# Key buffers in the sliding-window attention, output weights in halves, and the last norm on VectorE

## The chip, the cores and the metric

The kernel runs on one core of one Trainium2 chip. The metric is the device time of one execution in microseconds (us). Before the change it is 1278.24 us, the median of three runs (1277.53 to 1279.88).

## The reference

One decoder layer for a sequence of 1024 rows with 1024 columns, in float32. What is computed, cut to what matters here:

```
h    = rmsnorm(x) * (1 + sc1) + sh1              # sc1 .. g2 come from c @ w_ada
proj = h @ w_in                                  # columns for four groups of heads
o_sb = stick_breaking_attention(...)             # group 0
o_sw = sliding_window_attention(...)             # group 1: window 128, 4 query heads, 2 key heads
o_fx = forgetting_attention(...)                 # group 2
o_sm = s5_ssm(...)                               # group 3
mixed = rmsnorm per group of concat(o_sb, o_sw, o_fx, o_sm), each 256 wide
x = x + g1 * (mixed @ w_out)
h = rmsnorm(x) * (1 + sc2) + sh2
x = x + g2 * (square(relu(h @ w_mlp_in)) @ w_mlp_out)
return rmsnorm(x) * final_gain
```

## The kernel before

Products run on TensorE (PE) in three passes: each float32 operand is split into a high part (a rounded copy, made on ScalarE) and a low part (the difference, made on VectorE), and `mm3` adds high x high, high x low and low x high into one PSUM bank. PE, PEld, DVE, ACT, POOL and SP stand for TensorE's matmuls, its weight loads, VectorE, ScalarE, GpSimd and SyncE. The code is written in program order; a scheduler of the framework then sets the order in which each engine's instructions stand, and each engine takes them strictly in that order. SP issues nearly all loads and stores from one queue, again in a fixed order: an entry that has to wait for a buffer holds up every entry behind it.

Three places matter here.

The sliding-window attention (`sw_units`, from line 746) goes through eight units (j, p): j counts four pairs of row blocks, p the two key heads. For each j two key tiles `kk` (line 754, tag `kw`, two buffers in all) are loaded, one for each p (L756), and the query tiles `s` (L610). The scores are L733 on PE, their row maxima and exponentials L735 and L740. The units are mixed in with the end of the forgetting attention, with the projections of the groups 0 and 2 through `w_out` (L253 to L255 into `ps`, added to `x1` by L1029), and with the end of the state-space group (L831 to L913).

The output weights (`out_weights`, from line 969): for each of the groups 0, 2, 3 and 1, two blocks of 128 rows of `w_out` are loaded whole (128 x 1024, L975) into the tile `raw`, of which there is one buffer. VectorE multiplies the block by the gate g1 (L976), ScalarE copies the high part (L977), VectorE subtracts (L978). Only then is `raw` free for the next load. The squares of the second norm (`norm2`, L1139 and L98) use the same buffer.

The end: the last of 16 pieces of the hidden layer is multiplied for all eight row blocks t (the loop that calls `take` and `finish`). For each t and each half n, PE fills one bank with six matmuls, `take` adds it to `acc[t]` on VectorE (L1362), and `finish(t)` makes the last norm: squares with a running sum on ScalarE (L1385, by halves), a chain of six operations on 128 x 1 tiles on VectorE and two on ScalarE for the row factor (L1386, L86 to L92), and then the scaling by row factor and `final_gain`. For odd t VectorE does this in one instruction a half (L1390, `scalar_tensor_tensor`); for even t ScalarE scales (L1393) and GpSimd multiplies (L1394). Each half is stored by SP (L1395).

Of the kernel before, what the change touches and what calls it, by code (L numbers as in the profile page):

```python
# [9 lines left out]
F32 = mybir.dt.float32  # L10
F32R = mybir.dt.float32r
BF16 = mybir.dt.bfloat16
I32 = mybir.dt.int32
AF = mybir.ActivationFunctionType
ALU = mybir.AluOpType
# [4 lines left out]
P = 128  # L20
S = 1024
D = 1024
# [11 lines left out]
def tile_trunk(ctx: ExitStack, tc: tile.TileContext, a: dict, out: bass.AP):  # L34
    nc = tc.nc
    V, A, G, T, SY = nc.vector, nc.scalar, nc.gpsimd, nc.tensor, nc.sync
# [44 lines left out]
    def rsqrt_mean(pool, ss, n, width, tag, bufs=2):  # L81

        v = pool.tile([P, width], F32, name=f"{tag}v", tag=f"{tag}v", bufs=bufs)
        r = pool.tile([P, width], F32, name=f"{tag}r", tag=f"{tag}r", bufs=bufs)
        t = pool.tile([P, width], F32, name=f"{tag}t", tag=f"{tag}t", bufs=bufs)
        V.tensor_scalar(v, ss, 1.0 / n, EPS, op0=ALU.mult, op1=ALU.add)  # L86
        A.activation(r, v, AF.Ln)
        A.activation(r, r, AF.Exp, scale=-0.5)
        V.tensor_tensor(t, r, r, op=ALU.mult)
        V.tensor_tensor(t, t, v, op=ALU.mult)  # L90
        V.tensor_scalar(t, t, -0.5, 1.5, op0=ALU.mult, op1=ALU.add)
        V.tensor_tensor(r, r, t, op=ALU.mult)  # L92
        return r

    def norm_rows(pool, xt, sq, tag):

        ss = pool.tile([P, 1], F32, tag=f"{tag}ss", name="ss", bufs=2)
        A.activation(sq, xt, AF.Square, accum_out=ss)  # L98
        return rsqrt_mean(pool, ss, D, 1, tag)
# [1 line left out]
    WB, WA, XB, XQ = 5, 7, 4, 1  # L101
    RW, RC, LA, WS, FIRST, EB = 2, 6, 4, 2, 2, 4
    LB, RH = 2, 8
    FD_DVE, EL = (1, 3, 5, 7), 2
    MS = [5, 5, 5, 1]
    RC2 = max(MS) + LB + 1
    MARK = (1, 3)
# [497 lines left out]
    def load_q(qd, h, c0, c1):  # L605

        s = []
        for r in range(2):
            s.append(att.tile([P, c1 - c0], F32R, tag=f"s{r}", bufs=QB, name=f"s{r}"))
            load = SY.dma_start(out=s[r].bitcast(F32), in_=qd[h * HD:h * HD + HD, r:r + 2, c0:c1])  # L610
        return s, load.ins
# [112 lines left out]
    def sw_rows(q, kk, i, r, B, p):  # L724

        K = 256 if i else P
        z = ps1.tile([P, 2, 256], F32, tag="z", bufs=NZ, name="z")
        w = att.tile([P, 2, 256], F32, tag="t", bufs=3, name="w")
        m = att.tile([P, 4, 2], F32, tag="m", bufs=4, name="m")
        hs = slice(2 * p, 2 * p + 2)  # L730
        for x in range(2):
            for k in range(2):
                T.matmul(z[:, x, :], q[x][0][k][:, (i % 2) * P:(i % 2) * P + P], kk[:, 0:256],  # L733
                         start=k == 0, stop=k == 1)
            V.tensor_tensor_reduce(out=w[:, x, 0:K], in0=z[:, x, 0:K], in1=B[:, x, 256 - K:256], scale=1.0,  # L735
                                   scalar=-3e38, op0=ALU.add, op1=ALU.max, accum_out=m[:, 0, x:x + 1])
        V.scalar_tensor_tensor(out=m[:, 1], in0=m[:, 0], scalar=-1.0, in1=nsink[:, hs], op0=ALU.mult, op1=ALU.min)
        V.tensor_tensor(m[:, 2], m[:, 1], nsink[:, hs], op=ALU.subtract)
        for x in range(2):
            A.activation(w[:, x, 0:K], w[:, x, 0:K], AF.Exp, bias=m[:, 1, x:x + 1], accum_out=m[:, 3, x:x + 1])  # L740
        A.activation(m[:, 2], m[:, 2], AF.Exp)
        V.tensor_tensor(m[:, 3], m[:, 3], m[:, 2], op=ALU.add)
        V.reciprocal(r[:, i % 2], m[:, 3])
        return w

    def sw_units():

        B = [op.tile([P, 2, 256], F32, tag="B", bufs=2, name="B") for _ in range(2)]
        for b, t in enumerate(B):
            SY.dma_start(out=t, in_=BD[b])  # L750
        for j in range(4):
            k0 = max(2 * j - 1, 0) * P
            k1 = min(k0 + 384, S)
            kk = [op.tile([P, 384], F32R, tag="kw", bufs=2, name="kk") for _ in range(2)]
            for h in range(2):
                SY.dma_start(out=kk[h][:, 0:k1 - k0].bitcast(F32), in_=KD[2][h * HD:h * HD + HD, :, k0:k1])  # L756
            for p in range(2):
                q = [load_q(QD[2 + p], x, j * 256, j * 256 + 256) for x in range(2)]
                pv, r = None, att.tile([P, 2, 2], F32, tag="r", bufs=3, name="r")
                hs = slice(p * HD, p * HD + HD)  # L760
                for i in (2 * j, 2 * j + 1):
                    b0 = max(i - 1, 0)
                    w = sw_rows(q, kk[p][:, b0 * P - k0:], i, r, B[p], p)
                    ws = [[(w[:, x, (b - b0) * P:(b - b0 + 1) * P], b) for b in range(b0, i + 1)] for x in range(2)]
                    pv = mix(ws, v_sw, [hs, hs], i, pv, True)
                put(o_sw[:, 2 * j:2 * j + 2, p * P:p * P + P], pv, r)
                yield
# [198 lines left out]
    g1bc = op.tile([P, D], F32, name="g1bc")  # L966
    SY.dma_start(out=g1bc, in_=MD[2].to_broadcast([P, D]))

    def out_weights(g):

        h = op.tile([P, 2, D], F32R, tag="wo", bufs=4, name="woh")
        l = op.tile([P, 2, D], F32R, tag="wo", bufs=4, name="wol")
        for b in range(2):
            raw = op.tile([P, D], F32, tag="raw", bufs=1, name="raw")
            SY.dma_start(out=raw, in_=a["w_out"][0, g * 256 + b * P:g * 256 + b * P + P, :])  # L975
            V.tensor_tensor(raw, raw, g1bc, op=ALU.mult)  # L976
            A.copy(h[:, b], raw)  # L977
            V.tensor_tensor(l[:, b], raw, h[:, b], op=ALU.subtract)  # L978
        return h, l

    turns = [0]
# [70 lines left out]
    xts = [(xpa if n < 2 else xp).tile([P, 2, D], F32, name=f"x1_{n}") for n in range(4)]  # L1052
# [27 lines left out]
    def bank(kind):  # L1080
        n = used[kind] % 4
        used[kind] += 1
        pool, tag, bufs = ((ps2, "h", 3) if n < 3 else (psm, "ss", 1)) if kind == "x" else (
            (ps2, "t", 2) if n < 2 else (psm, "mm", 2))
        return pool.tile([P, 512], F32, tag=tag, bufs=bufs, name=kind)
# [49 lines left out]
    def norm2(j, y):  # L1135

        SY.dma_start(out=XD[j].rearrange("(t p) d -> p t d", p=P), in_=xts[j])
        for t in range(2):
            sq = op.tile([P, D], F32, tag="raw", bufs=1, name="sq")  # L1139
            r = norm_rows(op, xts[j][:, t], sq, "n2")  # L1140
            V.tensor_scalar(y[:, t], xts[j][:, t], r[:, 0:1], None, op0=ALU.mult)
        return [y[:, 0], y[:, 1]]

# [30 lines left out]
    for _ in range(FIRST):  # L1174
        x, z = bank("x"), bank("y")
        product(x, next_parts(), b11, True)
        product(z, next_parts(), b21, True)
        r = copy_of(x)
# [18 lines left out]
    for i in range(FIRST):  # L1197
        y = bank("y")
        product(y, next_parts(), t1, True)
        banks[i] += (y, copy_of(y))  # L1200
    for k, (u, b) in enumerate(zip(us, bs)):
        f = tt.tile([P, 512], F32, tag="f", bufs=2, name="f")
# [74 lines left out]
    for i in range(NP):  # L1277
        if i < FIRST:
            x, r, y, pe = banks[i]
            hidden(i, 0, r)  # L1280
        else:
            x, z, y = bank("x"), bank("y"), bank("y")
# [28 lines left out]
    sx = tc.alloc_tile_pool(name="sx", bufs=1, side="right", reuse_waits="tile")  # L1311
    acc = [sx.tile([P, D], F32, name=f"acc{t}") for t in range(NT)]
    g2bc = sx.tile([P, D], F32, name="g2bc")
    fg = sx.tile([P, D], F32, name="fg")
# [60 lines left out]
        V.tensor_tensor(acc[t][:, cs], acc[t][:, cs], g2bc[:, cs], op=ALU.mult)  # L1375
        V.tensor_tensor(acc[t][:, cs], acc[t][:, cs], rest_of[t][:, cs], op=ALU.add)

    def finish(t):

        y = acc[t]  # L1380
        ss = sx.tile([P, 2], F32, tag="n3ss", bufs=2, name="ss")
        halves = [slice(n * 512, n * 512 + 512) for n in range(2)]
        for n, cs in enumerate(halves):
            sq = sx.tile([P, 512], F32, tag="sq", bufs=2, name="sq")
            A.activation(sq, y[:, cs], AF.Square, accum_out=ss[:, n:n + 1])  # L1385
        V.tensor_tensor(ss[:, 0:1], ss[:, 0:1], ss[:, 1:2], op=ALU.add)  # L1386
        r = rsqrt_mean(sx, ss[:, 0:1], D, 1, "n3")
        for n, cs in enumerate(halves):
            if t in FD_DVE:
                V.scalar_tensor_tensor(out=y[:, cs], in0=y[:, cs], scalar=r[:, 0:1], in1=fg[:, cs],  # L1390
                                       op0=ALU.mult, op1=ALU.mult)
            else:
                A.activation(y[:, cs], y[:, cs], AF.Copy, scale=r[:, 0:1])  # L1393
                G.tensor_tensor(y[:, cs], y[:, cs], fg[:, cs], op=ALU.mult)  # L1394
            SY.dma_start(out=out[t * P:(t + 1) * P, cs], in_=y[:, cs])  # L1395

    last = load_raw(chunks[0], (0, 2, 1, 3)).ins
    for _ in range(RH):
# [28 lines left out]
    for t in range(NT):  # L1427
        for n in range(2):
            ps = bank("x" if n else "y")
            for x in range(2):  # L1430
                h = ha[2 * x + t // 4]
                ts = slice(t % 4 * P, t % 4 * P + P)
                mm3(ps, (h[0][:, ts], h[1][:, ts]), wa[2 * x + n], x == 0, x == 1)
            take(c, t, n, ps)
        finish(t)
    sr.release()
    sc.release()
    sr1.release()
# [52 lines left out]
```

## Time and profile before

| | |
|---|---|
| median of three runs | 1278.24 us |
| profiled execution | 1281.41 us, of which span 1279.3 us |
| PE busy | 1214.4 us (95%) |
| VectorE busy | 955.3 us (75%) |
| ScalarE busy | 562.4 us (44%) |
| GpSimd busy | 125.3 us (10%) |
| mean granted clock of TensorE | 0.976 of full speed |

The span runs from the first to the last instruction of the profiled execution; about 2.1 us lie around it. The clock is given as a share of the full 2.4 GHz; the other level is 1.2 GHz, 0.5. Matmuls are pipelined, so an instruction's own duration (0.39 us for one of 512 columns) is longer than the distance to the next (0.23 us). On VectorE, too, the distance between two independent instructions is shorter than the duration of one.

### The profile page before, as it was taken

How to read it: one execution, taken by the hardware profiler on the slowest of the kernel's cores; microseconds unless marked ns; L12 is line 12 of the kernel's file. 1: busy time of each engine (PE TensorE's matmuls, PEld its weight loads, DVE VectorE, ACT ScalarE, POOL GpSimd, SP SyncE). 2: the span in 40 equal slices, each digit the busy share in tenths (PEclk: the TensorE clock that was granted, in tenths of full speed). 3: DMA queues.
4: the chain of work that ended last, by engine and by line, in shares of the span. 5: the costliest groups of instructions: out<-in, count | busy, mean ns of one | idle time of the engine just before them, and what ended most of it. 6: DMA issues, size and time to landing. Idle time of an engine off the chain costs nothing.

```text
span 1279.3 us, 18741 instructions
## 1 busy us (share of the span) xinstructions
PE 1214.4 (95%) x6461; PEld 945.6 (74%) x6461; DVE 955.3 (75%) x2100; ACT 562.4 (44%) x1205; POOL 125.3 (10%) x171
## 2 busy tenths in 40 slices
PE   5899899999999998999899999999989999999994
PEld 3578677665677776888668888888867888888883
DVE  4685977775465687888998677767666777788998
ACT  4433555762224557545563232333344543433425
POOL 1218100000020100000000000000031210100003
PEclk9999899999999898999989999999999999999997
DMA  8664376576654655202124553443578653643413
GB/s 297 201 198 146 139 195 212 175 221 185 215 175 153 238 152 175 88 26 83 67 66 166 172 167 131 155 154 130 170 250 315 213 168 108 182 127 91 138 48 132
DMA packets 139334, 205.37 MB, mean 161 GB/s; under 512 B 37057, under 2 KB 77912, under 8 KB 139240
## 3 DMA queue, kind: packets, MB, share of 16 engines
q1 hardware_dynamic: 129768, 170.62, 41.6%
q0 software_dynamic: 9472, 33.56, 8.4%
q8 instruction: 51, 0.84, 0.3%
q14 instruction: 43, 0.35, 0.1%
HBM read 144.59 MB, written 59.55 MB: 160 GB/s over the span
## 4 chain that ended last, share of the span: by engine, by line
PE 80%; DVE 8%; DMA 7%; ACT 2%; issue 2%; SPq 1%; DVEq 0%; ACTq 0%
PE x L255 9%; PE x L253 9%; PE x L254 8%; PE y L254 6%; PE y L255 6%; PE y L253 6%; PE ps L253 6%; PE ps L254 6%; PE ps L255 6%; PE pv L705 3%; PE tp L700 3%; PE z L639 3%; PE ps L307 2%; DMA wa<-in_w_ada_dram 2%; DMA kk<-kd 1%
## 5 line engine op out<-in xcount | busy, mean ns | idle before, releaser
L1091 ACT CAST hi<-s 128x512 fp32r<-128x512 f32 x124 | 75.9, 618 | 110.8 <-PE x L254 36.7
L1091 ACT CAST hi<-hid 128x512 fp32r<-128x512 f32 x101 | 62.2, 618 | 129.7 <-issue 58.1
L254 PE MATMUL x<-lo,hi 128*128 128x512 f32 x256 | 98.3, 389 | 0.3 <-DVE lo L1092 0.3
L253 PE MATMUL x<-hi 128*128 128x512 f32 x256 | 95.9, 390 | 2.4 <-ACT hi L1091 2.4
L255 PE MATMUL x<-hi,lo 128*128 128x512 f32 x256 | 97.8, 389 | 0.0
L1092 DVE TENSOR_TENSOR lo<-raw,hi 128x512 fp32r<-128x512 f32 x97 | 65.9, 686 | 40.8 <-PE x L255 21.6
L253 PE MATMUL ps<-hT_hi,wh 128*128 128x512 f32 x224 | 90.8, 417 | 4.9 <-DVE e L273 2.6
L255 PE MATMUL ps<-hT_hi,wl 128*128 128x512 f32 x224 | 91.5, 411 | 1.5 <-DVE wl L185 1.5
L1091 ACT CAST hi<-raw 128x512 fp32r<-128x512 f32 x97 | 59.1, 619 | 74.2 <-PE y L254 45.9
L254 PE MATMUL ps<-hT_lo,wh 128*128 128x512 f32 x224 | 91.2, 408 | 0.0
L1092 DVE TENSOR_TENSOR lo<-s,hi 128x512 fp32r<-128x512 f32 x124 | 84.2, 684 | 3.1 <-ACT hi L1091 2.1
L1092 DVE TENSOR_TENSOR lo<-hid,hi 128x512 fp32r<-128x512 f32 x101 | 69.1, 685 | 21.1 <-ACT hi L1091 19.0
L255 PE MATMUL y<-hi,lo 128*128 128x512 f32 x196 | 75.3, 389 | 0.0
L254 PE MATMUL y<-lo,hi 128*128 128x512 f32 x196 | 75.2, 389 | 0.0
L253 PE MATMUL y<-hi 128*128 128x512 f32 x196 | 73.6, 390 | 0.3 <-ACT hi L1091 0.3
L700 PE MATMUL tp<-ident,w 128*128 128x128 f32 x348 | 60.3, 288 | 5.7 <-ACT w L666 5.5
L703 DVE COPY wt<-tp 128x512 f32<-128x512 f32 (+1 forms) x68 | 42.8, 638 | 27.2 <-PE tp L700 25.7
L1273 POOL DMA_DIRECT2D raw<-in_w_mlp_out_dram x64 | 34.4, 540 | 258.6 <-DVE lo L1092 75.1
L1099 POOL DMA_DIRECT2D raw<-in_w_mlp_in_dram x16 | 14.4, 898 | 453.9 <-DVE lo L1092 384.9
L253 PEld LDWEIGHTS x<-hi 128*128 128x128 f32 x256 | 48.0, 188 | 13.1 <-ACT hi L1091 3.2
L639 PE MATMUL z<-kk,s 128*128 128x256 f32 (+2 forms) x192 | 55.2, 382 | 2.5 <-DMA kk<-kd 2.5
L700 PEld LDWEIGHTS tp<-ident,w 128*128 128x128 f32 x348 | 40.0, 144 | 23.8 <-issue 11.2
(416 smaller groups left out, 3261.2 us busy)
## 6 DMA issues: line engine op xcount, KB each, us to landing
hid<-hh SPq DMA_DIRECT2D x101, 256.0 KB
wa<-in_w_ada_dram SPq DMA_DIRECT2D x32, 512.0 KB
raw<-in_w_mlp_in_dram POOLq DMA_DIRECT2D x16, 1024.0 KB, 7.0
raw<-in_w_mlp_out_dram POOLq DMA_DIRECT2D x64, 256.0 KB, 4.5
hh<-x SPq DMA_DIRECT2D x60, 256.0 KB
hh<-h SPq DMA_DIRECT2D x49, 256.0 KB
s<-qd SPq DMA_DIRECT2D x96, 128.0 KB
wa<-in_w_ada_dram SPq DMA_DIRECT2D x32, 256.0 KB
```

The costliest lines, as they stand in the source:

```text
L253: T.matmul(ps, wh, xh, start=first, skip_group_check=more, stop=False)
L254: T.matmul(ps, wh, xl, start=False, skip_group_check=more, stop=False)
L255: T.matmul(ps, wl, xh, start=False, skip_group_check=more, stop=last)
L307: T.matmul(ps[32 * r:32 * r + 1, :], cact[:, k:k + 1], w[:, n * 512:(n + 1) * 512], start=k == 0, stop=k == KT - 1)
L639: T.matmul(z[:, 0:n], q[r][:, qs], kk[:, 0:n], start=r == 0, stop=stop and r == 1)
L700: T.transpose(tp[:, b, :], w, ident)
L703: (A.copy if copies[0] % 2 and both else V.tensor_copy)(wt[:, 0:len(part)], tp[:, 0:len(part)])
L705: T.matmul(pv[x * HD:x * HD + HD, i % 2, :], v[:, kb, hs[x]], wt[:, b, :], start=n == 0, stop=n == len(ws[0]) - 1)
L1091: A.copy(shape(hi), src)
L1092: V.tensor_tensor(shape(lo), src, shape(hi), op=ALU.subtract)
L1099: G.dma_start(out=raws[i].rearrange("p (k c) -> p k c", k=KT), in_=w1[:, i * 256:i * 256 + 256].rearrange("(k p) c -> p k c", p=P))
L1273: load = G.dma_start(out=raw2[i, kind], in_=w2[(2 * i + x) * P:(2 * i + x + 1) * P, n * 512:n * 512 + 512])
```

## The change

1. `sw_units`: the key tiles `kk` have three buffers instead of two. A tile is then free for its next load when the scores of the unit three loads earlier are done, not two loads earlier.
2. `out_weights`: each block is loaded, multiplied, copied and subtracted in two halves of 512 columns, and `raw` has two buffers of half the size. `norm2` squares in two halves too, and adds the two sums.
3. `finish`: all eight row blocks are scaled on VectorE by `scalar_tensor_tensor`; ScalarE's scaling and GpSimd's multiplication are gone. The row factors of two blocks are made by one chain on 128 x 2 tiles for the pairs (0, 1), (2, 3), (4, 5); the blocks 6 and 7 have a chain each.

```
-            kk = [op.tile([P, 384], F32R, tag="kw", bufs=2, name="kk") for _ in range(2)]
+            kk = [op.tile([P, 384], F32R, tag="kw", bufs=3, name="kk") for _ in range(2)]
...
-            raw = op.tile([P, D], F32, tag="raw", bufs=1, name="raw")
-            SY.dma_start(out=raw, in_=a["w_out"][0, g * 256 + b * P:g * 256 + b * P + P, :])
-            V.tensor_tensor(raw, raw, g1bc, op=ALU.mult)
-            A.copy(h[:, b], raw)
-            V.tensor_tensor(l[:, b], raw, h[:, b], op=ALU.subtract)
+            for n in range(2):
+                ns = slice(n * 512, n * 512 + 512)
+                raw = op.tile([P, 512], F32, tag="raw", bufs=2, name="raw")
+                SY.dma_start(out=raw, in_=a["w_out"][0, g * 256 + b * P:g * 256 + b * P + P, ns])
+                V.tensor_tensor(raw, raw, g1bc[:, ns], op=ALU.mult)
+                A.copy(h[:, b, ns], raw)
+                V.tensor_tensor(l[:, b, ns], raw, h[:, b, ns], op=ALU.subtract)
...
-            sq = op.tile([P, D], F32, tag="raw", bufs=1, name="sq")
-            r = norm_rows(op, xts[j][:, t], sq, "n2")
+            ss = op.tile([P, 2], F32, tag="n2ss", bufs=2, name="ss")
+            for n in range(2):
+                sq = op.tile([P, 512], F32, tag="raw", bufs=2, name="sq")
+                A.activation(sq, xts[j][:, t, n * 512:n * 512 + 512], AF.Square, accum_out=ss[:, n:n + 1])
+            V.tensor_tensor(ss[:, 0:1], ss[:, 0:1], ss[:, 1:2], op=ALU.add)
+            r = rsqrt_mean(op, ss[:, 0:1], D, 1, "n2")
...
-    def finish(t):
+    def finish(ts):
...
+        n = len(ts)
+        ss = sx.tile([P, 2, 2], F32, tag="n3ss", bufs=2, name="ss")
+        for x, t in enumerate(ts):
+            for h in range(2):
+                sq = sx.tile([P, 512], F32, tag="sq", bufs=2, name="sq")
+                A.activation(sq, acc[t][:, h * 512:h * 512 + 512], AF.Square, accum_out=ss[:, h, x:x + 1])
+        V.tensor_tensor(ss[:, 0, 0:n], ss[:, 0, 0:n], ss[:, 1, 0:n], op=ALU.add)
+        r = rsqrt_mean(sx, ss[:, 0, 0:n], D, n, f"n3{n}")
+        for x, t in enumerate(ts):
+            for h in range(2):
+                cs = slice(h * 512, h * 512 + 512)
+                y = acc[t][:, cs]
+                V.scalar_tensor_tensor(out=y, in0=y, scalar=r[:, x:x + 1], in1=fg[:, cs], op0=ALU.mult, op1=ALU.mult)
+                SY.dma_start(out=out[t * P:(t + 1) * P, cs], in_=y)
...
-        finish(t)
+        if t % 2 or t == 6:
+            finish({1: (0, 1), 3: (2, 3), 5: (4, 5)}.get(t, (t,)))
```

The scheduler's order is the same up to the first of the new loads and again in the two MLP products; it differs from there to the second norm and in the end. Three places follow.

First, SP's queue while the sliding-window units run. Before the change, `kk_5700`, the key tile of the unit j=2, p=0, stands behind the queries of the unit after its own (`s0_5776` to `s0_5780`) and between the stores of the state-space group's third and second output piece (`o_4065`, `o_4080`):

```order
L913 DMA od2_74<-o_4065 128x256
L913 DMA od3_75<-o_4065 128x256
L610 DMA s0_5776<-qd3_64 128x1x256
L610 DMA s1_5778<-qd3_64 128x1x256
L610 DMA s0_5780<-qd3_64 128x1x256
L756 DMA kk_5700<-kd2_69 128x384
L913 DMA od0_72<-o_4080 128x256
L913 DMA od1_73<-o_4080 128x256
L610 DMA s1_5782<-qd3_64 128x1x256
```

After the change the same entry stands directly behind the queries of the unit j=1, p=1 (`s0_5632`, `s1_5634`) and ahead of the first store of the state-space group (`o_4050`):

```order
L977 DMA raw_6536<-in_w_out_dram 128x512
L977 DMA raw_6541<-in_w_out_dram 128x512
L610 DMA s0_5632<-qd3_64 128x1x256
L610 DMA s1_5634<-qd3_64 128x1x256
L756 DMA kk_5700<-kd2_69 128x384
L913 DMA od0_72<-o_4050 128x256
L913 DMA od1_73<-o_4050 128x256
L610 DMA s0_5704<-qd2_63 128x1x256
L913 DMA od2_74<-o_4065 128x256
L913 DMA od3_75<-o_4065 128x256
L610 DMA s1_5706<-qd2_63 128x1x256
L610 DMA s0_5708<-qd2_63 128x1x256
```

The load has moved ahead of four stores and seven loads of queries that stood in front of it, and it now waits for the scores of unit j=0, p=1 instead of those of unit j=1, p=0.

Second, VectorE's order where the second block of group 3's weights is made. Before the change, the multiplication of the whole block stands 23 rows behind the subtraction that frees its buffer; these are the last ten of them:

```order
L92 TENSOR_TENSOR gnr<-gnr,gnt 128x2
L742 TENSOR_TENSOR m<-m 128x2
L721 TENSOR_TENSOR o_sw<-pv,rb 128x2x128
L743 RECIPROCAL r<-m 128x2
L735 ISA w,m<-z,B 128x256
L735 ISA m 128x1
L715 COPY rw<-r 128x256
L735 ISA w,m<-z,B 128x256
L735 ISA m 128x1
L976 TENSOR_TENSOR raw<-raw,g1bc 128x1024
```

After the change, the multiplication of the first half (L978 there) stands eleven rows behind the two subtractions (L980) that free the two buffers:

```order
L980 TENSOR_TENSOR wol<-raw,woh 128x512 x2
L735 ISA w,m<-z,B 128x256
L735 ISA m 128x1
L735 ISA w,m<-z,B 128x256
L735 ISA m 128x1
L742 TENSOR_TENSOR m<-m 128x2
L721 TENSOR_TENSOR o_sw<-pv,rb 128x2x128
L86 TENSOR_SCALAR gnv<-ps 128x2
L737 SCALAR_TENSOR_TENSOR m<-m,nsink 128x2
L743 RECIPROCAL r<-m 128x2
L738 TENSOR_TENSOR m<-m,nsink 128x2
L978 TENSOR_TENSOR raw<-raw,g1bc 128x512
```

Less of VectorE's work stands between the freeing of the buffer and the use of what is loaded into it.

Third, the end of VectorE's order (`acc_9864` and `acc_9866` are the row blocks 5 and 7). Before the change the chains of the row factors of blocks 6 and 7 run side by side, and only block 7 is scaled here:

```order
L1390 SCALAR_TENSOR_TENSOR acc_9864<-acc_9864,n3r,fg 128x512 x2
L1386 TENSOR_TENSOR ss<-ss 128x1
L89 TENSOR_TENSOR n3t<-n3r 128x1
L86 TENSOR_SCALAR n3v<-ss 128x1
L90 TENSOR_TENSOR n3t<-n3t,n3v 128x1
L91 TENSOR_SCALAR n3t<-n3t 128x1
L92 TENSOR_TENSOR n3r<-n3r,n3t 128x1
L89 TENSOR_TENSOR n3t<-n3r 128x1
L90 TENSOR_TENSOR n3t<-n3t,n3v 128x1
L91 TENSOR_SCALAR n3t<-n3t 128x1
L92 TENSOR_TENSOR n3r<-n3r,n3t 128x1
L1390 SCALAR_TENSOR_TENSOR acc_9866<-acc_9866,n3r,fg 128x512 x2
```

After the change (`acc_9929` and `acc_9930` are the blocks 6 and 7) the scaling of block 6 stands inside the chain of block 7:

```order
L1392 TENSOR_TENSOR ss<-ss 128x1
L89 TENSOR_TENSOR n31t<-n31r 128x1
L86 TENSOR_SCALAR n31v<-ss 128x1
L90 TENSOR_TENSOR n31t<-n31t,n31v 128x1
L91 TENSOR_SCALAR n31t<-n31t 128x1
L92 TENSOR_TENSOR n31r<-n31r,n31t 128x1
L89 TENSOR_TENSOR n31t<-n31r 128x1
L1398 SCALAR_TENSOR_TENSOR acc_9929<-acc_9929,n31r,fg 128x512 x2
L90 TENSOR_TENSOR n31t<-n31t,n31v 128x1
L91 TENSOR_SCALAR n31t<-n31t 128x1
L92 TENSOR_TENSOR n31r<-n31r,n31t 128x1
L1398 SCALAR_TENSOR_TENSOR acc_9930<-acc_9930,n31r,fg 128x512 x2
```

Directly in front of these rows now stand the four scalings of the blocks 4 and 5, and in front of those the two `take`s of block 7.

## Rows read from the trace of the kernel before

**Rows 1.** The page: busy time by engine, and the chain's shares.

```profile
PE 1214.4 (95%) x6461; PEld 945.6 (74%) x6461; DVE 955.3 (75%) x2100; ACT 562.4 (44%) x1205; POOL 125.3 (10%) x171
PE 80%; DVE 8%; DMA 7%; ACT 2%; issue 2%; SPq 1%; DVEq 0%; ACTq 0%
```

**Rows 2.** Windows: length, busy PE, PEld, DVE, ACT, POOL (count), granted clock, DMA, GB/s.

```profile
500.00:520.00 20.00, 13.99 (x79) 11.35 (x78) 9.11 (x39) 10.10 (x34) 0.00 (x0) 0.74 0.57 188
520.00:560.00 40.00, 39.86 (x281) 32.62 (x282) 32.72 (x122) 21.25 (x69) 0.00 (x0) 1.00 0.19 57
560.00:600.00 40.00, 38.96 (x196) 31.93 (x194) 36.43 (x99) 20.78 (x54) 0.00 (x0) 1.00 0.25 86
600.00:640.00 40.00, 36.12 (x176) 28.05 (x176) 37.52 (x87) 20.46 (x43) 0.00 (x0) 0.98 0.14 53
...
1263.00:1280.00 17.00, 0.00 (x0) 0.00 (x0) 12.06 (x31) 6.19 (x18) 5.87 (x4) 0.59 0.47 173
```

**Rows 3.** Waits of PE from 395 to 645 us: total us, times, longest.

```profile
PE z L733 <- DMA kk<-kd: 5.8, 1, 5.8
```

**Rows 4.** Timeline of PE, 500 to 516 us: start, us, engine, instruction, idle before.

```profile
508.72 1.19 PE L733 MATMUL z<-kk,s 128*128 128x256 f32 x4 [5.79 <-DMA kk<-kd]
...
513.55 0.63 PE L255 MATMUL ps<-woh,ml 128*128 128x512 f32 x1
...
515.45 0.40 PE L254 MATMUL ps<-wol,mh 128*128 128x512 f32 x1
```

**Rows 5.** Timeline of SP's queue, 496 to 512 us.

```profile
500.49 0.56 SPq L756 DMA_DIRECT2D kk<-kd  x1
...
509.94 0.33 SPq L756 DMA_DIRECT2D kk<-kd  x1
```

**Rows 6.** Timeline of POOL, 494 to 512 us (two loads of 1 MB each).

```profile
497.86 1.98 POOL L1099 DMA_DIRECT2D raw<-in_w_mlp_in_dram  x2 [69.06 <-ACT mh L1014]
```

**Rows 7.** The chain that ended last, 395 to 660 us: start, us, what.

```profile
500.49 8.10 DMA kk<-kd
...
526.65 4.51 DMA raw<-in_w_out_dram
...
535.04 3.61 DMA raw<-in_w_out_dram
```

**Rows 8.** Timeline of DVE, 518 to 542 us.

```profile
524.41 1.21 DVE L978 TENSOR_TENSOR wol<-raw,woh 128x1024 fp32r<-128x1024 f32 x1
...
531.19 1.23 DVE L976 TENSOR_TENSOR raw<-raw,g1bc 128x1024 f32<-128x1024 f32 x1 [0.87 <-DMA raw<-in_w_out_dram]
```

**Rows 9.** Groups of instructions, 1240 to 1280 us: count | busy us, mean ns | idle before.

```profile
L1390 DVE SCALAR_TENSOR_TENSOR acc<-acc,n3r,fg 128x512 f32<-128x512 f32 x8 | 13.9, 1779 | 0.1
L1394 POOL TENSOR_TENSOR acc<-acc,fg 128x512 f32<-128x512 f32 x8 | 11.8, 1502 | 73.0 <-ACT acc L1393 73.0
L1385 ACT ACTIVATE sq<-acc 128x512 f32<-128x512 f32 x16 | 10.0, 624 | 12.9 <-DVE acc L1362 12.9
...
L1362 DVE TENSOR_TENSOR acc<-acc,x 128x512 f32<-128x512 f32 x9 | 6.1, 682 | 1.1 <-PE x L255 0.9
```

**Rows 10.** Timeline of PE, 1260 to 1264 us.

```profile
1260.79 0.39 PE L255 MATMUL y<-hi,lo 128*128 128x512 f32 x1
...
1262.15 0.39 PE L255 MATMUL x<-hi,lo 128*128 128x512 f32 x1
```

**Rows 11.** Timeline of DVE, 1236 to 1280 us.

```profile
1252.49 3.53 DVE L1390 SCALAR_TENSOR_TENSOR acc<-acc,n3r,fg 128x512 f32<-128x512 f32 x2
1255.94 0.68 DVE L1362 TENSOR_TENSOR acc<-acc,y 128x512 f32<-128x512 f32 x1
...
1271.96 3.50 DVE L1390 SCALAR_TENSOR_TENSOR acc<-acc,n3r,fg 128x512 f32<-128x512 f32 x2
```

**Rows 12.** Timeline of DVE, 496 to 512 us.

```profile
498.19 0.68 DVE L834 SCALAR_TENSOR_TENSOR sgm<-sgm,mid 128x512 f32<-128x512 f32 x1
498.79 0.48 DVE L1015 SCALAR_TENSOR_TENSOR ml<-v_fx,cols,mh 128x256 fp32r<-128x256 f32 x1
```

More of the change, by code (lines that the diff above doesn't have):

```diff
@@ L103, in tile_trunk @@
     LB, RH = 2, 8
-    FD_DVE, EL = (1, 3, 5, 7), 2
+    EL = 2
     MS = [5, 5, 5, 1]
@@ L1376, in gated @@
         V.tensor_tensor(acc[t][:, cs], acc[t][:, cs], rest_of[t][:, cs], op=ALU.add)
-    def finish(t):
[L1380 to L1395, printed above, removed]
+    def finish(ts):
[13 more added lines that the diff above has]
+                SY.dma_start(out=out[t * P:(t + 1) * P, cs], in_=y)
     last = load_raw(chunks[0], (0, 2, 1, 3)).ins
```

## The prediction

> **What bounds the kernel now.** I read the page first: PE is busy for 95% of the span and carries 80% of the chain that ended last [rows 1]. So time is won only where PE waits or runs slowly, and after its last matmul. The windows say where that is [rows 2]. From 500 to 520 us PE is busy for 13.99 of 20 us at a granted clock of 0.74. From 520 to 560 it has no gap to speak of (39.86 of 40) and VectorE has slack (32.72). From 560 to 640 both are close to full: PE 38.96 and 36.12 of 40, VectorE 36.43 and 37.52. In the last 17 us PE does nothing and VectorE works 12.06.
>
> The waits name the first hole: PE waits once, for 5.8 us, for a key tile of the sliding-window attention [rows 3]. SP issued that load at 500.49 [rows 5], and it took 8.10 us to land [rows 7], because GpSimd had put two loads of 1 MB each in front of it at 497.86 [rows 6]. PE goes on at 508.72 [rows 4], and what follows costs more than the wait: 512-column matmuls last 0.63 us at 513.55 and 0.40 at 515.45. A mean of 0.74 over 20 us, between the levels 1.2 GHz (0.5) and 2.4 GHz, is (1 - 0.74) x 2 = 52% of the stretch at 1.2, some 10.4 us. About 6.5 us of these, from 508.72 to about 515.2, hold work; the rest lies in the wait.
>
> The second hole is the end. PE's last matmul starts at 1262.15 [rows 10]; VectorE ends at 1271.96 + 3.50 = 1275.46 [rows 11], and the span at 1279.3.
>
> **Keys in three buffers.** The load of the key tile for unit j=2, p=0 waits today for the scores of unit j=1, p=0 and stands late in SP's queue. With three buffers it waits for unit j=0, p=1, and it stands ahead of four stores and seven loads that it used to follow. Only one thing in front of it can still hold it: the loads of the output weights, which wait for VectorE's subtractions in turn. The corresponding ones stand in front of it in today's order too, far ahead of its issue at 500.49 [rows 5], so I expect the load to leave before GpSimd's two large ones at 497.86. Then the wait of 5.8 us goes, and with it the reason for the low clock: the 6.5 us of work at 1.2 GHz shrink by half, 3.2 us. Together 9.0 us. The next tile, j=2, p=1, was issued at 509.94 [rows 5]; it will be issued around 502, amid the 2 MB, land at about 509, and PE asks for it some 12 us after the first, at about 514.
>
> What is late next? ScalarE and VectorE also used those 5.8 us to catch up: between 500 and 520 ScalarE was busy for 10.10 us. PE now asks for their squares and exponentials earlier. The new order on PE puts 24 projection matmuls (24 x 0.23 = 5.5 us) around the place, which need nothing new, so I charge 1 us, between 0 and the whole 5.8.
>
> **Output weights in halves.** The work is the same: one multiplication and one subtraction of 1024 columns take 1.23 and 1.21 us [rows 8], two halves of 512 columns at a distance of 0.60 each [rows 11, 12] take 1.2. The new thing is the wait for the load. Today the multiplication stands 23 rows behind the subtraction, starts 6.8 us after it and still waits 0.87 us for the load [rows 8]. In the new order 10 rows stand between; at today's mean of (6.8 - 1.21 - 0.87) / 22 = 0.21 us a row they fill 2.1 us, and the second subtraction 0.6 more, but no addition of a projection is among them, so I take 2. A whole block took 4.51 and 3.61 us to land [rows 7]; the half lies between nothing and 4.51, and I take 4, as there are two halves in flight. That makes VectorE wait about 2 us there, near 520. Behind it on VectorE stand the additions of the projection's results (L1029) and the maxima of the scores, which free PE's banks; VectorE has 7 us of slack in the 40 us after 520 [rows 2], so I let 1 us of it through to PE. Three other pairs are as close; those before 500 and the one near 540 I take as hidden by the same slack, and the last one, near 575, stands where VectorE is nearly full, for another 0.5 us. Sum for the halves: 1.5 us lost, between 0 and some 4. The extra squares of the second norm are on ScalarE, which is busy for half of that time (20.78 of 40), and cost nothing.
>
> Here a rule speaks against the halves. The Trainium skill, "DMA: Bandwidth & Descriptors", section on the anatomy of one DMA, gives each transfer a fixed part of about 2.0 us, whatever its size, so halving pays it twice. By its fit an estimate for 256 KB is 2.6 us and for 512 KB 3.2; the trace has 3.61 and 4.51 for the latter [rows 7], more than the rule. With 2.6 instead of 4 the first wait would be 0.6 us instead of 2 and the middle about 1 us better.
>
> Sum for the middle: 9.0 - 1.0 - 1.5 = 6.5 us gained. From 680 on PE has no gaps and the order is the old one, so the whole product moves forward by that.
>
> **The end.** Today eight scalings on VectorE have a mean of 1779 ns [rows 9], in pairs of about 3.5 us, always beside GpSimd's multiplication of the same shape (1502 ns). The same kind of instruction on SBUF tiles, 128 x 512, takes 0.68 us where GpSimd is idle, and the next one starts 0.60 us later [rows 12]. I take 0.60 as the distance; 1.73 is the other end. From the first pair at 1252.49 to 1275.46 are 22.97 us: four pairs take 13.7 (from start to start of what follows, 1252.49 to 1255.94 for the first [rows 11]), eight `take`s at 0.60 take 4.8, and 4.5 are small operations and waits. After the change: sixteen scalings 9.6, eight `take`s 4.8, and 4.2 for small operations and waits (fewer chains, but about 1.5 us of waiting for PE's banks, which come every 1.36 us [rows 10], and the last chain of block 7 in the open). That is 18.6 us, an end at 1271.1, 4.4 us earlier. It can't be much earlier: from PE's last matmul a `take`, two squares, the chain and two scalings follow, and the four scalings of blocks 4 and 5 stand between. Squares are not a bound: 16 of them take 10.0 us on ScalarE [rows 9].
>
> **Sum.** 6.5 + 4.4 = 10.9 us less than the profiled execution's 1281.41, so 1270.5. That execution lies 3.2 us above the median of the runs, 1278.24; I lay the sum on the median: 1267.3 us.
>
> **Rivals.**
> *Another wait takes the place of the first.* For it: ScalarE's backlog, and the second key tile in the middle of the 2 MB. Against it: the projections that PE has to do there. The middle then gives 1 to 2 us instead of 6.5, and the clock stays low: 1278.2 - 1.5 - 4.4 = 1272.3. Chance 0.14.
> *The end is ruled by something else.* If a chain or a store ends last as late as today, the middle alone gives 1271.7. Against it: VectorE's last scaling starts 9.8 us behind PE's last matmul [rows 10, 11], and the changed work is VectorE's own. Chance 0.05.
> *More is won.* From 600 to 640 PE idles for 3.9 us, where VectorE is nearly full [rows 2]; if the new order closes that, 1263.4, and less if the clock gains too. Against it: VectorE's work there stays the same. Chance 0.08.
> *Slower: the scaling is slow by itself.* All eight rows of this form stand beside GpSimd, so the trace doesn't separate the two. At a distance of 1.73 us the sixteen take 27.7 instead of 9.6 us; less the 1.5 us of waiting that this swallows, VectorE ends at 1287.7, 12.2 us later than today, and with the middle's gain the kernel takes 1284. It decides from 1.4 us per scaling on, where the loss at the end eats up the middle. Against it stands the row of 0.68 us for the same kind without `final_gain` [rows 12]. The Trainium skill, "GPSIMD Engine Reference", section on key points, says that GpSimd shares its SBUF interfaces with VectorE and gets in the way of instructions with two SBUF inputs; by that the 1.78 us are GpSimd's doing and the rival is out. Chance 0.04.
> *Slower or level by the order.* The halves cost their full 4 us and the first rival comes too. Chance 0.03 beyond those above.
>
> **Chances and range.** Forecast 0.66; the five rivals 0.14, 0.05, 0.08, 0.04 and 0.03. About 0.2% (2.6 us) is what a measurement of this kernel can tell from no change. Nearly all of the first three rivals is faster by more, the forecast wholly: faster 0.88, within 0.2% 0.05, slower 0.07. The forecast's own spread is 1263 to 1271 (the middle between 3 and 9, the end between 3 and 6). The range reaches up to the first two rivals and down to the third: 1260.5 to 1274.
>
> **What would show it.** Right: no wait of PE for a key tile from 480 to 530, a clock of 1.0 from 500 to 520, VectorE waiting near 520 and 575 for the weights' halves by 0 to 2 us each, scalings of 0.68 us at the end and VectorE's last instruction about 9 us after PE's last start. Wrong: the key tile still landing behind GpSimd's loads, a fall of the clock in another place between 430 and 640, PE waiting for squares or exponentials near 505, or scalings above 1.4 us.

## The result, and the profile after

The changed kernel takes 1265.68 us (median of six runs, 1258.67 to 1269.01) beside 1277.88 us for the kernel before on the same chip: a ratio of 0.9900 with an interval of 0.9878 to 0.9921. In a second measurement, beside the experiments below, it had 0.9913 [0.9888, 0.9938]. The forecast was 1267.3 us. The runs of either kernel lie up to 10 us apart, so a single profile says little about a few us; the experiments have to.

The profiled execution of the changed kernel took 1263.04 us, with a span of 1261.3. Its page has PE busy for a larger share of a shorter span and on more of the chain, and DMA on 4% of the chain instead of 7% [rows 1]:

```profile
PE 1206.2 (96%) x6461; PEld 939.9 (75%) x6461; DVE 951.7 (75%) x2114; ACT 559.4 (44%) x1215; POOL 112.8 (9%) x163
PE 84%; DVE 7%; DMA 4%; issue 1%; ACT 1%; SPq 1%; DVEq 0%; ACTq 0%
```

Windows of the changed kernel, columns as in [rows 2]:

```profile
480.00:500.00 20.00, 18.49 (x110) 13.88 (x109) 16.49 (x63) 15.51 (x47) 1.98 (x2) 0.95 0.59 183
500.00:520.00 20.00, 20.00 (x137) 16.58 (x135) 17.31 (x70) 11.35 (x40) 0.00 (x0) 0.97 0.54 176
520.00:560.00 40.00, 39.83 (x258) 32.60 (x258) 33.40 (x104) 21.03 (x62) 0.00 (x0) 1.00 0.07 21
560.00:600.00 40.00, 38.63 (x191) 32.02 (x190) 36.15 (x112) 20.08 (x64) 0.00 (x0) 1.00 0.25 93
600.00:640.00 40.00, 36.03 (x169) 28.17 (x168) 37.77 (x79) 25.53 (x50) 0.88 (x1) 0.91 0.08 29
```

The hole at 500 us is filled: PE is busy for 20.00 of 20 us at a clock of 0.97 instead of 13.99 at 0.74. What is new stands just before it. From 480 to 500 PE idles for 1.5 us, and the clock there is 0.95. The stretch from 600 to 640 has changed little. Its clock, 0.91 instead of 0.98, comes from the window's edge: both profiles have 6.8 us at the low level there, from 624.2 us now and from 638.0 before.

SP's queue in the changed kernel (the two key tiles of j=2, and two of the weights' halves), and GpSimd's:

```profile
474.93 0.58 SPq L756 DMA_DIRECT2D kk<-kd  x1
492.35 0.54 SPq L756 DMA_DIRECT2D kk<-kd  x1
...
508.01 0.34 SPq L977 DMA_DIRECT2D raw<-in_w_out_dram  x1
...
516.67 0.33 SPq L977 DMA_DIRECT2D raw<-in_w_out_dram  x1
```

```profile
492.00 1.98 POOL L1101 DMA_DIRECT2D raw<-in_w_mlp_in_dram  x2 [67.18 <-PE z L733]
```

The tile that PE used to wait for now leaves 17 us before GpSimd's two loads, where it left 2.6 us behind them [rows 5, 6]. The second one is issued amid the 2 MB. From 480 to 645 us the longest waits of PE are these, and no key tile is among them or the shorter ones:

```profile
PE ps L193 <- ACT b L1189: 2.0, 1, 2.0
PE ps L253 <- ACT woh L979: 1.4, 1, 1.4
PE z L733 <- DVE m L735: 1.3, 1, 1.3
PE ps L193 <- DVE e L1185: 1.1, 1, 1.1
```

The third stands in front of the low clock near 500. The timeline of PE has it at

```profile
495.85 0.50 PE L733 MATMUL z<-kk,s 128*128 128x256 f32 x2 [1.26 <-DVE m L735]
```

and the clock's record, which the windows average, falls to half from 497.9 to 501.3 us.

The end, first PE's last matmul, then VectorE's scalings in the timeline, then their groups from 1230 us on (count | busy us, mean ns | idle before):

```profile
1248.35 0.39 PE L255 MATMUL x<-hi,lo 128*128 128x512 f32 x1
```

```profile
1251.23 2.74 DVE L1398 SCALAR_TENSOR_TENSOR acc<-acc,n32r,fg 128x512 f32<-128x512 f32 x4
1254.81 1.41 DVE L1398 SCALAR_TENSOR_TENSOR acc<-acc,n31r,fg 128x512 f32<-128x512 f32 x2
...
1256.70 1.41 DVE L1398 SCALAR_TENSOR_TENSOR acc<-acc,n31r,fg 128x512 f32<-128x512 f32 x2
```

```profile
L1398 DVE SCALAR_TENSOR_TENSOR acc<-acc,n32r,fg 128x512 f32<-128x512 f32 x12 | 8.2, 748 | 0.1
L1398 DVE SCALAR_TENSOR_TENSOR acc<-acc,n31r,fg 128x512 f32<-128x512 f32 x4 | 2.8, 746 | 0.0
```

A scaling has a mean of 748 ns instead of 1779 [rows 9], and in a run of four the distance is (2.74 - 0.75) / 3 = 0.66 us. VectorE ends at 1256.70 + 1.41 = 1258.11, 9.8 us behind the start of PE's last matmul; before it was 13.3 [rows 10, 11]. From that start to the end of the span it is now 12.95 us (1261.3 - 1248.35) instead of 17.15 (1279.3 - 1262.15).

### The profile page after: what moved, and what is told of

Same layout as the page of the kernel before. It is cut to its first block, busy times and chain, and to the rows that moved or that the text cites. A ratio compares the mean times of both kernels' runs of the same rounds, so it can differ in the third digit from the quotient of the medians.

```text
span 1261.3 us, 18773 instructions
## 1 busy us (share of the span) xinstructions
PE 1206.2 (96%) x6461; PEld 939.9 (75%) x6461; DVE 951.7 (75%) x2114; ACT 559.4 (44%) x1215; POOL 112.8 (9%) x163
## 3 DMA queue, kind: packets, MB, share of 16 engines
q1 hardware_dynamic: 130920, 170.63, 41.9%
## 4 chain that ended last, share of the span: by engine, by line
PE 84%; DVE 7%; DMA 4%; issue 1%; ACT 1%; SPq 1%; DVEq 0%; ACTq 0%
PE x L255 9%; PE x L253 9%; PE x L254 9%; PE ps L253 7%; PE y L254 7%; PE y L255 7%; PE y L253 7%; PE ps L254 6%; PE ps L255 6%; PE pv L705 4%; PE tp L700 4%; PE z L639 3%; PE ps L307 2%; DMA hid<-hh 1%; DMA xt<-in_x_dram 1%
## 5 line engine op out<-in xcount | busy, mean ns | idle before, releaser
L639 PE MATMUL z<-kk,s 128*128 128x256 f32 (+2 forms) x192 | 55.8, 383 | 1.8 <-DMA kk<-kd 1.8
L255 PEld LDWEIGHTS ps<-hT_hi,wl 128*128 128x128 f32 x224 | 43.4, 194 | 17.9 <-issue 5.6
L254 PEld LDWEIGHTS x<-lo,hi 128*128 128x128 f32 x256 | 48.0, 188 | 10.6 <-DVE lo L1094 0.7
```

Of the source, the lines that this page charges most:

```text
L254: T.matmul(ps, wh, xl, start=False, skip_group_check=more, stop=False)
L255: T.matmul(ps, wl, xh, start=False, skip_group_check=more, stop=last)
L639: T.matmul(z[:, 0:n], q[r][:, qs], kk[:, 0:n], start=r == 0, stop=stop and r == 1)
```

## The experiments

Each ran in six to twelve executions beside the kernel before. The first four shared a chip, the next four another, and the last three a third; before had medians of 1277.72, 1277.91 and 1277.66 us. The ratio is the recorded one, of the runs beside each other, and not the quotient of the two medians: for the keys the ratio says 12 us and the medians 9.7. "Low clock" is the time at 1.2 GHz, worked out from the mean granted clock c of all the runs of a kernel as (1 - c) x 2 x mean span. In before it is 52.4 us, a mean over 62 runs, and 13 of these lie in the tail of the profiled one, where PE has no work.

```
what is in it          median us  ratio [interval]          low clock us
before                 1277.7     1                         52.4
keys                   1268.04    0.9905 [0.9875, 0.9934]   39.6
norm                   1273.80    0.9961 [0.9945, 0.9977]   47.1
halves                 1277.47    0.9996 [0.9977, 1.0014]   49.1
keys, halves           1271.55    0.9945 [0.9924, 0.9965]   48.7
keys, norm             1262.63    0.9884 [0.9856, 0.9912]   34.1
keys, norm, again      1263.41    0.9896 [0.9877, 0.9914]   40.0
halves, norm           1273.92    0.9970 [0.9953, 0.9987]   46.6
all (the change)       1266.87    0.9913 [0.9888, 0.9938]   43.8
all, when first run    1265.68    0.9900 [0.9878, 0.9921]   40.0
no GpSimd product      1272.26    0.9951 [0.9933, 0.9970]   47.3
loads behind           1270.47    0.9942 [0.9924, 0.9961]   42.7
keys, norm, squares    1261.87    0.9887 [0.9865, 0.9909]   35.7
```

**The keys alone.**

```diff
-            kk = [op.tile([P, 384], F32R, tag="kw", bufs=2, name="kk") for _ in range(2)]
+            kk = [op.tile([P, 384], F32R, tag="kw", bufs=3, name="kk") for _ in range(2)]
```

> The kernel before with the key tiles in three buffers and nothing else. The prediction's theory: the load of the key tile for j=2, p=0 leaves before GpSimd's two loads of 1 MB, PE's wait of 5.8 us goes, and the low clock behind it too: 8.0 us less than before (between 3 and 9), ratio about 0.9937; no wait of PE for a key tile between 480 and 530 us. Rival, another wait takes the place: ScalarE's and VectorE's backlog or the next key tile holds PE instead, 1 to 2 us less, ratio about 0.9988. Rival, it needs the halves too: with the weights' whole rows in one buffer SP's queue stands still, the key tile is still issued behind GpSimd's loads, and the time is that of before within 0.2%.

Measured: 1268.04 us, 0.9905 [0.9875, 0.9934], by the ratio 12 us less. Both rivals fall: no other wait takes the place, and the halves aren't needed for it. From 480 to 530 us the list of PE's waits is empty, and the window reads

```profile
500.00:520.00 20.00, 19.88 (x145) 16.31 (x144) 18.13 (x73) 13.99 (x45) 0.15 (x1) 1.00 0.72 227
```

The gain is larger than expected. The last column of the table may hold a part of the reason: 12.8 us less at the low clock, where the prediction took away the 10.4 of one place. By the spread of the runs this mean is good to some 5 us (twice its standard error), so it isn't shown that more than the one place changed. 3.8 us of these lay inside the old wait and cost nothing (the clock's record has it low from 504.9, PE goes on at 508.72); the other 9.0 held work and are worth half, 4.5 us. With the wait of 5.8 that makes 10.3, within the interval.

**The norm alone.**

```diff
-            if t in FD_DVE:
-                V.scalar_tensor_tensor(out=y[:, cs], in0=y[:, cs], scalar=r[:, 0:1], in1=fg[:, cs],
-                                       op0=ALU.mult, op1=ALU.mult)
-            else:
-                A.activation(y[:, cs], y[:, cs], AF.Copy, scale=r[:, 0:1])
-                G.tensor_tensor(y[:, cs], y[:, cs], fg[:, cs], op=ALU.mult)
+                V.scalar_tensor_tensor(out=y, in0=y, scalar=r[:, x:x + 1], in1=fg[:, cs], op0=ALU.mult, op1=ALU.mult)
```

> The kernel before with the new last norm and nothing else (all scalings on VectorE, row factors of two blocks at once). The prediction's theory: 4.4 us less, ratio 0.9966; from the trace of the changed kernel, where VectorE's last instruction ends 9.8 us after PE's last start instead of 13.3, 3.5 to 4.2. Scalings at about 0.75 us instead of 1.78. Rival, the scaling is slow by itself: 12 us more. Rival, the end hangs on the stores: no gain, ratio 1.000.

Measured: 1273.80 us, 0.9961 [0.9945, 0.9977], 5 us less. From PE's last start (1259.51) to the end of the span (1272.5) it is 12.99 us, as in the whole change; the keys alone have 17.17 (1267.0 - 1249.83), as before. The other profiles with the new norm have 13.0 to 13.2 us there. So the end is worth some 4.2 us wherever it stands, and a scaling has 748 ns.

**The halves alone.**

```diff
-            raw = op.tile([P, D], F32, tag="raw", bufs=1, name="raw")
...
+            for n in range(2):
+                ns = slice(n * 512, n * 512 + 512)
+                raw = op.tile([P, 512], F32, tag="raw", bufs=2, name="raw")
...
+                sq = op.tile([P, 512], F32, tag="raw", bufs=2, name="sq")
```

> The kernel before with the output weights' raw rows and the second norm's squares in halves with two buffers, and nothing else. The prediction's theory: the work is the same and VectorE waits more for the loads: 1.5 us more than before (between 0 and 4), ratio 1.0012; PE's wait of 5.8 us for a key tile stays. Rival, the halves are where the middle's gain comes from: SP's queue is held for a shorter time behind VectorE's subtractions, the key tile is issued earlier, and the time is 3 to 6 us less, ratio 0.9953 to 0.9977.

Measured: 1277.47 us, 0.9996 [0.9977, 1.0014]: no difference. PE's wait for the key tile is shorter here, 3.17 us instead of 5.79, since that tile is issued at 497.67, 0.7 us behind GpSimd's loads at 496.93, where it was 2.6. The low clock behind it is shorter too, 3.4 us instead of 10.2. So a cost of the halves elsewhere would be hidden by what they take off this wait, and the experiment doesn't price them.

**GpSimd's multiplications left out.**

```diff
                 A.activation(y[:, cs], y[:, cs], AF.Copy, scale=r[:, 0:1])
-                G.tensor_tensor(y[:, cs], y[:, cs], fg[:, cs], op=ALU.mult)
```

> The kernel before without GpSimd's eight multiplications by the final gain (half of the output rows are left without that factor); ScalarE's and VectorE's scalings stay as they are. Theory: a scaling takes 1.78 us on VectorE because GpSimd multiplies beside it. Then the eight scalings take 0.68 to 0.75 us, VectorE's four pairs 1.4 instead of 3.5 us, and the end comes 4 to 8 us earlier, ratio 0.994 to 0.997. Rival, the scaling with three operands in this tile is slow by itself: 1.78 us as before, and at most 1.5 us (GpSimd's last multiplication) are saved.

Measured: 1272.26 us, 0.9951 [0.9933, 0.9970]. The group of VectorE's scalings, whose code is that of before:

```profile
L1390 DVE SCALAR_TENSOR_TENSOR acc<-acc,n3r,fg 128x512 f32<-128x512 f32 x8 | 5.7, 748 | 0.1
```

On every other engine the order is that of before. With nothing changed but GpSimd's work beside it, the same instruction falls from 1779 to 748 ns. The rival, a form that is slow by itself, is out. (Half of the output rows lack `final_gain` here, so the time is that of less work.)

**The parts together.** The changed kernel again; without the new norm; without the halves; without the third buffer:

```
all:           key tiles bufs=3, raw rows and squares in halves, finish(ts)
keys, halves:  without finish(ts)
keys, norm:    without the halves
halves, norm:  key tiles bufs=2
```

> The changed kernel again, beside the next three on one chip. Alone on the kernel before, the keys gave a ratio of 0.9905, the norm 0.9961, the halves 0.9996; their product is 0.9862, the whole change had 0.9900 [0.9878, 0.9921]. Theory one, the parts add up: 0.9862 here. Theory two, the halves cost 3 to 5 us where the keys no longer wait: 0.9895 to 0.991. Theory three, the keys alone came out too well in six runs: 0.989 to 0.990, and the kernel with keys and norm the same.

> The kernel before with the key tiles in three buffers and the halves, and its old last norm. Theory one, the parts add up: 0.9905 x 0.9996 = 0.9901. Theory two, the halves cost 3 to 5 us beside the keys: 0.993 to 0.9945. Theory three, the keys came out too well: 0.992 to 0.9935, and then the kernel with keys and norm has 0.989 to 0.990.

> The changed kernel without the halves: key tiles in three buffers and the new last norm. Theory one, the parts add up: 0.9905 x 0.9961 = 0.9866, as the whole change within 0.15%. Theory two, the halves cost beside the keys: 0.9866, 3 to 5 us below the whole change. Theory three, the keys came out too well: 0.989 to 0.990, as the whole change.

> The changed kernel with its key tiles in two buffers: halves and new last norm alone. All theories: 0.9996 x 0.9961 = 0.9957. If the halves' order by itself lets the key tile land earlier (PE waited 3.2 us for it instead of 5.8 with the halves alone), the wait is 3.2 us here too and the granted clock from 490 to 520 us above 0.74.

Measured: 0.9913, 0.9945, 0.9884, 0.9970. Theory two comes nearest: the kernel with keys and norm is 4.2 us below the whole change beside it on one chip, keys alone 3.5 us (by the ratios 5) below keys and halves. It isn't met in full: 0.9884 lies between its 0.9866 and the 0.989 of theory three, and 0.9913 just above its range. The parts don't add up, since two of them meet in one place: the third buffer gives 10 to 12 us where the rows are whole (0.9905; 0.9884 against 0.9961) and 6.5 to 7.3 by the ratios where they are in halves (0.9945 against 0.9996; 0.9913 against 0.9970). Without keys and with the halves PE waits 2.23 us for the key tile, less than the 3.2 expected, but the clock of that place is as low as in before (0.80 from 490 to 515 us in both).

Where the halves differ is in the trace. Windows of keys and halves, and of keys and norm:

```profile
490.00:510.00 20.00, 18.24 (x116) 14.49 (x116) 15.61 (x57) 13.01 (x38) 1.98 (x2) 0.91 0.63 205
```

```profile
490.00:510.00 20.00, 19.88 (x126) 15.73 (x125) 16.91 (x65) 14.13 (x42) 1.98 (x2) 1.00 0.69 227
```

In every profile with keys and halves (three of them) PE waits 1.2 to 1.3 us there for VectorE's maximum (L735) and the clock falls; in every one with keys and whole rows (four, with those below) neither happens. The low clock of all runs points the same way: 9.1 us more in keys and halves than in keys alone, worth at most 4.6; 4.9 us more in the whole change (41.9 over both measurements) than in keys and norm (37.0), and that with a tail some 0.8 us shorter, worth at most 2.9. By the runs' spread these two differences are good to 6 and 5 us only. The means of the runs differ by 5.0 and 2.5 us, and by their spread these are good to 2.8 and 2.2 us (the first lies across two chips, whose means of before are 0.6 us apart). That the halves cost something beside the keys is shown by this; that the wait at 494 and the clock behind it are the whole cost is argued, since no run takes away that wait alone.

**GpSimd's loads behind the key tile.** In the kernel before, GpSimd reads one column of the tile for j=2, p=0 before it issues its two loads; on PE, VectorE, ScalarE and SP every instruction keeps its place.

```diff
                 SY.dma_start(out=kk[h][:, 0:k1 - k0].bitcast(F32), in_=KD[2][h * HD:h * HD + HD, :, k0:k1])
+            if j == 2:
+                seen = op.tile([P, 1], F32, tag="seen", bufs=1, name="seen")
+                G.tensor_copy(seen, kk[0][:, 0:1].bitcast(F32))
```

> The kernel before (key tiles in two buffers) with one small instruction more: GpSimd copies one column of the key tile for j=2, p=0 before it issues its two loads of 1 MB. So these leave after that tile has landed; on every other engine each instruction stands where it stood. Theory, the tile was late because the 2 MB were in front of it: it lands 2 to 3 us after its issue instead of 8.10, PE waits 0 to 1 us for it instead of 5.8, the 10.2 us of low clock behind the wait go or shrink to 3.4, and the time is 7 to 10 us less, ratio 0.992 to 0.9945, nearly what the third buffer alone gives (0.9905). Rival, it is late by its issue at 500.49 alone: PE waits 4 us or more as before, ratio 0.998 to 1.000. Rival, the loads of 2 MB are missed later by PE: a wait for them near 550 us, ratio 0.996 or more.

Measured: 1270.47 us, 0.9942 [0.9924, 0.9961], 7 us less. Timelines of SP, GpSimd and PE, and the load on the chain that ended last:

```profile
497.85 0.86 SPq L756 DMA_DIRECT2D kk<-kd  x1
```

```profile
501.43 0.18 POOL L759 COPY seen<-kk 128x1 f32<-128x1 f32 x1 [76.69 <-DMA od<-o]
502.04 1.98 POOL L1102 DMA_DIRECT2D raw<-in_w_mlp_in_dram  x2 [0.43 <-PE z L733]
```

```profile
501.23 0.70 PE L733 MATMUL z<-kk,s 128*128 128x256 f32 x4 [0.94 <-DMA kk<-kd]
```

```profile
497.85 3.25 DMA kk<-kd
```

Issued at its old place in SP's order, the tile lands in 3.25 us instead of 8.10 [rows 7], and PE waits 0.94 us. Beside PE's work the issue hasn't moved: PE stops 2.44 us behind it in both kernels (at 500.29 here and 502.93 before, the starts less the waits). So it was the 2 MB in front that made the tile late, not its issue alone, and PE has no wait for the 2 MB later. The two rivals fall. The clock still drops for 3.4 us after this wait (from 503.6), and the gain is 7.4 by the ratio, the lower end of what was expected.

**Only the squares in halves.** Keys and norm, with the weights' rows whole and the squares in two parts of the same tile:

```diff
+            sq = op.tile([P, D], F32, tag="raw", bufs=1, name="sq")
+            for n in range(2):
+                A.activation(sq[:, n * 512:n * 512 + 512], xts[j][:, t, n * 512:n * 512 + 512], AF.Square, accum_out=ss[:, n:n + 1])
```

> The kernel with key tiles in three buffers and the new last norm, and of the halves only those of the second norm's squares (the weights' raw rows stay whole, in one buffer). Without the halves that kernel had 0.9884, with all of them 0.9913 and 0.9900. Theory, the weights' halves are what costs, through the wait of PE of 1.3 us near 494 and the low clock behind it: 0.988 to 0.989 here, no fall of the clock between 480 and 520 us. Rival, the new order that the squares bring costs: 0.990 to 0.9915.

> Key tiles in three buffers and the new last norm without the halves, again: 0.9884 [0.9856, 0.9912] the first time. If the halves cost 3 to 5 us it is 0.9865 to 0.989 again, below the whole change's 0.9900 and 0.9913; if the first was chance, 0.990 to 0.991.

Measured: 1261.87 us, 0.9887 [0.9865, 0.9909], and keys and norm again 1263.41, 0.9896 [0.9877, 0.9914], between the two outcomes that were expected of it. No cost of the squares shows; the clock is 1.00 from 480 to 520. What is left as the cost is the weights' rows in halves, with the order that they bring. Both kernels, without those halves, are the fastest of the study; by the medians they lie 2 to 5 us below the whole change, by the intervals of the ratios, which overlap, the least of that isn't certain.

## Why the prediction was right, and where it was not

The time was right (1265.68 and 1266.87 against 1267.3), and the mechanism of both holes. Two terms of the sum were too small, the gain of the keys and the cost of the halves, and that they cancelled was luck.

- *The key tile.* As forecast: issued before GpSimd's loads, the wait of 5.8 us gone, the clock up. That the 2 MB were the cause, and not the late issue alone, is shown by the kernel that changes nothing but their order. The next tile was issued amid the 2 MB, as forecast, though at 492.35 instead of about 502, and cost nothing.
- *The clock.* The step priced one place, 6.5 us of work at half speed, and took 3.2 us. Over all runs the means give 9.0 us and 4.5, good to some 5 us of clock, so that this is the term that was too small isn't shown. The records of single profiles have low stretches near 413 and between 432 and 443 us that some executions show and some don't, with two buffers and with three; where the rest of the keys' gain comes from wasn't settled.
- *The backlog, 1 us.* About right. With the time that work lost at half speed taken out, the stretch from the first score of the forgetting attention (L639) after 395 us to the last sliding-window score (L733) is 136.7 us long in before (144.99 less half of the 16.7 us of work at the low clock) and 131.6 with the keys alone: 5.0 of the 5.8 us came through. The profiles of the kernels with norm alone and without GpSimd's multiplications, whose order there is that of before, give 4.0 and 4.2. Another wait of PE in this stretch, for a key tile of the forgetting attention (L639), is 0.6 to 2.5 us long in these four profiles, so each figure is good to a us or two.
- *The halves, 1.5 us, up to some 4.* Mis-sized: 2.5 and 5 us by the means where the keys are there. The step looked for the cost on VectorE near 520 and 575, in waits for the loads. Those are small: 0.79 and 0.39 us in the rows below, none for a load near 562. A half, issued at 508.01, had its multiplication waiting until 510.79, so it landed in some 2.8 us; the one of 516.67 in 3.0. I had taken 4. (The Trainium skill, "DMA: Bandwidth & Descriptors", section on the anatomy of one DMA, gives for a transfer that GpSimd issues a fixed part of about 2.0 us, by which my estimate for 256 KB was 2.6. The two loads here, issued by SP, lie 0.2 and 0.4 us above it.)

```profile
510.79 0.69 DVE L978 TENSOR_TENSOR raw<-raw,g1bc 128x512 f32<-128x512 f32 x1 [0.79 <-DMA raw<-in_w_out_dram]
...
519.66 0.69 DVE L978 TENSOR_TENSOR raw<-raw,g1bc 128x512 f32<-128x512 f32 x1 [0.39 <-DMA raw<-in_w_out_dram]
```

  What the profiles show instead lies earlier, at 494, and is no wait for a load at all: in the new order PE asks there for a maximum of VectorE 1.3 us too soon, and the clock falls behind it. The prediction had named "a fall of the clock in another place between 430 and 640" as a sign of being wrong, but charged nothing for it.
- *The end, 4.4 us.* It is 4.2. The distance is 0.66 us and not 0.60, which is 16 x 0.06 = 1.0 us more, and VectorE ends 9.8 us behind PE's last start, where the sum has 8.9 (1271.1 - 1262.15). The stores gave most of that back: the span ends 3.2 us behind VectorE instead of 3.8.
- *The scaling.* 748 ns, where 680 was forecast, and by the kernel without GpSimd's multiplications it was GpSimd that made it 1779. The prediction's row of 0.68 us [rows 12] was misread in one point: GpSimd wasn't idle there but issued its two loads, from 497.86 to 499.84 [rows 6]. The same line has 0.68 us at 492.46 too, before those loads, so issuing them didn't slow VectorE; multiplying did. (The Trainium skill, "GPSIMD Engine Reference", section on key points, has VectorE's instructions with two SBUF inputs disturbed by GpSimd; the two rows agree, and they size it: 2.4 times.)
- *The rivals.* None came, but a small form of the first did: a wait took the place of the old one, 1.3 us instead of 5.8 and in front of it instead of behind, and only because of the halves.

Against the sum: keys 10 to 12 instead of 8.0, halves 2.5 to 5 lost instead of 1.5, the end 4.2 instead of 4.4. The whole was forecast at 10.9 and measured 12.2 and 11.0 by the medians.

## What to carry to other kernels

Before a small load that is late gets another buffer, look at what stands in front of it on the DMA engines: here one tiny instruction that held back two large loads gave 7 of the 10 to 12 us without moving anything else. Price a wait of PE with the low clock behind it, and a new wait of 1 us likewise. A change of several parts is worth taking apart even when it wins: the part that looked free (rows in halves, the same work) took back a quarter to two fifths of what another had gained.

## What the runs showed of the hardware

The low clock near a wait isn't in proportion to it. In the profiles it lasted 10.2 us at waits of 5.8 us (three kernels), where it set in 2 us after PE had stopped, and 10.2 us too in the kernel with halves and norm, whose wait is 2.23 us and where it set in 2.4 us before it, behind three short waits of 0.56, 0.23 and 0.45 us. At waits of 3.17, 1.26 and 0.94 us it was 3.4 us, and set in some 3 us after PE had stopped. Between runs of one kernel the mean clock differs as well: in before the slowest run, 1285.50 us, has 0.975 and the fastest, 1272.87 us, 0.983, the ends of what its runs show.

A scaling of two SBUF tiles on VectorE (128 x 512) took 748 ns alone, 1779 ns beside GpSimd's multiplications, and the like one of rows 12 took 0.68 us beside GpSimd's issuing of loads. A load of 192 KB that was issued 2.6 us behind two of 1 MB landed in 8.10 us, and in 3.25 us with those two held back.
